# Two orders of work in a hybrid attention layer on one core: the place of one Strassen product in every pair, and the pairing of the last head's projections

## The chip, the cores and the metric

The kernel runs on one core of one Trainium2 chip. The metric is device microseconds of that core, from one launch; the median of several runs is taken. TensorE (PE in the views) does the matrix products, VectorE (DVE), ScalarE (ACT) and GpSimd (POOL) the elementwise work, SyncE (SP) issues most transfers, and POOL issues those that add to what lies in SBUF.

## The reference, cut to what matters

```python
u = rms_norm(h, norm_w)                       # 528 tokens (16 meta + 512) x 2048
proj = einsum('btd,de->bte', u, w_in)         # 2048 -> 8192 = 64 blocks of 128 columns
sb_q, sb_k, sb_v, sb_g, df_q, df_k, df_v, df_g = split(proj)   # 8 blocks (heads) each
# stick-breaking head: z = q k^T / sqrt(128); a = sigmoid(z) * running product of sigmoid(-z); o = a v
# differential head: two 64-wide softmax maps (rms norm and partial rotary on q, k), p0 - lam * p1; o = a v
mixed = concat([sb_o * silu(sb_g), subln(df_o) * silu(df_g)])
h = h + einsum('bte,ed->btd', mixed, w_out)   # 2048 -> 2048
```

Everything is float32. Queries and gates are needed for the 512 real tokens only, keys and values for all 528.

## The kernel before, in words

**Products.** A float32 product is three fp32r matmuls: each operand is split into a high part (an ACT copy, `L124`) and the rest (a DVE subtraction, `L125`), and high x high, high x low, low x high are summed in PSUM (`mm`, lines 279 to 281). Two 128-column blocks make a *pair*, and a pair is computed by a Strassen-Winograd scheme: both the weights (quadrants `a11`, `a12`, `a21`, `a22`) and the tokens (two halves) are cut in two, and seven products replace eight. The seven are called after their weights: `a11`, `a12`, `a22` as they lie, and the sums `s1` to `s4`. Each product is 8 (input side) or 7 (output side) contraction steps of 3 matmuls. `STEPS` says which PSUM bank a product goes to: `s1` to d, `a11` to a, `a12` to b, `a22` to c, `s4` to e; `s2` and then `s3` go on adding in bank a. Between `s2` and `s3` bank a has to be read: DVE adds bank d's copy to it and keeps the result as `ev_u` (line 523), and only then may PE add `s3` to the bank.

**Weights.** A pair's four quadrants come from HBM into six buffers `wr`. On the input side the sums are made by transfers that POOL issues and that add a quadrant to what lies in a buffer (`w_add`, line 174): `s1` in `a21`'s buffer right after its load, then `s2` in the same buffer once `s1` has been split, `s4` once `s2` has been split, and `s3` in `a11`'s buffer. On the output side POOL adds (line 220). A generator (`preps`, through `uses(s)`) splits each product's weights in the same order in which `proj_pair` uses the products. Each product's weights are split in two halves, and there are four buffers each for the high and low halves, so the splits run at most two products ahead of PE.

**Order.** `pairs()` lists the 32 pairs on the input side, four for each of the 8 heads (a *period*): for heads 0 to 6 differential key/value, differential query/gate, stick-breaking key/value, stick-breaking query/gate. Pairs named `..kv` are 264 columns wide per half (all 528 tokens), the others 256. Eight pairs on the output side follow: pair 32 is computed without Strassen (`direct`) while the mixed rows are read back from DRAM and split (`spread`, `combine`: tiles `uth`, `utl`, from `mr..`, `cos_t`, `sin_t`); pairs 33 to 39 are Strassen again, 7 steps deep, with a `plain` part for the last two heads, whose rows never go to DRAM.

Attention is woven into the products by `Pace`: each head is a generator that yields costs, and each step of a projection (`PACE` = 0.218 units) lets it run on. A differential head's scores `df_s` lie in two PSUM tiles in turn, so its third and later scores wait until `Exp` (line 838) has read the one before the last. In the last period (head 7) the pairs are differential key/value (28), both queries (29), stick-breaking key/value (30), both gates (31). The last differential head starts after pair 29; the stick-breaking head (`Tail`) may run only once the differential head has reached its value product (`projected`), and most of it runs inside pair 32. Pair 31's `s4` is computed at the end of its own pair; every other pair's `s4` is carried into the next pair.

A scheduler then places the instructions on each engine by its own timeline, within these dependences.

Of the kernel before, what the change touches and what calls it, by code (L numbers as in the profile page):

```python
# [2 lines left out]

# [1 line left out]

# [21 lines left out]
NH = 8  # L27
# [4 lines left out]
PACE = 0.218  # L32
# [27 lines left out]
def pairs():  # L60


    o = []
    for h in range(NH - 1):
        o += [("d_kv", h, 48 + h, 40 + h), ("d_qg", h, 56 + h, 32 + h)]
        o += [("s_kv", h, 16 + h, 8 + h), ("s_qg", h, 24 + h, h)]

    h = NH - 1
    o += [("d_kv", h, 48 + h, 40 + h), ("qq", h, h, 32 + h), ("s_kv", h, 16 + h, 8 + h), ("gg", h, 24 + h, 56 + h)]
    return o  # L70


# [10 lines left out]
def build(nc, tc, ctx, hT, win, wout, wpl, xT, prm, cst, out):  # L83
# [18 lines left out]
    def st_tile(name):  # L102
        return ww.tile([P, T], F32, tag="st", name=name, bufs=5)
# [31 lines left out]
    last_in = len(pairs()) - 1  # L135
# [90 lines left out]

    def uses(s):

        o = [(s, which) for which in ("s1", "a11", "a12", "a22", "s2", "s3")]
        if s - 1 > 1 and s - 1 not in (last_in, last_in + 1):  # L230
            o.insert(2, (s - 1, "s4"))
        if s in (last_in, len(plan) - 1):
            o.append((s, "s4"))
        return o

    def preps():
# [93 lines left out]
    for j, k in enumerate(order_h):  # L330
# [6 lines left out]
        x = ht[k]  # L337
# [348 lines left out]
        split(sk[:, 0], sk[:, 1], rk_)  # L686
        kst.append(sk)

    def sb_head(hd, kst, rv, rq_, rg):
        nm = f"sb{hd}"  # L690
        sk = kst[0]
        kh, kl = sk[:, 0], sk[:, 1]
        qh, ql = (sp.tile([P, SEQ], F32R, tag=f"dq{j}", name=f"{nm}_q{j}") for j in range(2))
        split(qh, ql, rq_[:, META:])
        yield 2
        for i in range(NB):
            n, view, spans, diag = s_views(ps_at(f"{nm}_s{i}"), i)
            qs = slice(i * P, (i + 1) * P)
            for j, (o, cs) in enumerate(spans):
                PE.matmul(o, qh[:, qs], kh[:, cs], start=True, stop=False)  # L700
                if j == len(spans) - 1:
                    PE.matmul(diag[0], msb, diag[1], start=False, stop=False)
                PE.matmul(o, qh[:, qs], kl[:, cs], start=False, stop=False)
                PE.matmul(o, ql[:, qs], kh[:, cs], start=False, stop=True)  # L704
            keep = w1_tile(f"{nm}_k{i}")[:, :n]
            beta = w3_tile(f"{nm}_b{i}")[:, :n]
            S.activation(sview(keep, i), view, AF.Sigmoid, scale=nrqs[:, i:i + 1])  # L707
            S.activation(sview(beta, i), view, AF.Sigmoid, scale=rqs[:, i:i + 1])  # L708
            run = sh_tile(f"{nm}_r{i}")[:, :n]
            V.tensor_tensor_scan(run[:, ::-1], keep[:, ::-1], ones_t.to_broadcast([P, n]), 1.0,  # L710
                                 op0=ALU.mult, op1=ALU.mult)
            V.tensor_tensor(a_t[i][:, :n - 1], beta[:, :n - 1], run[:, 1:], op=ALU.mult)  # L712
            V.memset(a_t[i][:, n - 1:n], 0.0)
            yield 1.5 if i < 3 else 2.5
        vh, vl = v_tiles(rv, nm)
        yield 1
        res = []
        last = hd == NH - 1
        yield from pv_product(vh, vl, nm, res, lambda: gate(rg[0], nm, w1_tile), hd == NH - 1, last)
        po, gs = res  # L720
        V.tensor_tensor(gs, po, gs, op=ALU.mult)
        mixed(hd, gs)
        yield 1
# [90 lines left out]
        kst.append(dk)  # L814
        yield 1

    def diff_head(hd, kst, rv, rq_, rg):
        nm = f"df{hd}"
        qst = []
        yield from diff_q(hd, rq_, qst)  # L820
# [2 lines left out]
        for i in range(NB):  # L823
            qs = slice(i * P, (i + 1) * P)
            pts = []
            sums = sp.tile([P, 2], F32, tag="sums", name=f"{nm}_sum{i}", bufs=2)
            for c in range(2):
                n, view, spans, diag = s_views(ps_at(f"{nm}_s{i}{c}"), i)
                for j, (o, cs) in enumerate(spans):
                    PE.matmul(o, qst[c][:, qs], dk[:, c, cs], start=True, stop=False)  # L830
                    if j == len(spans) - 1:
                        PE.matmul(diag[0], mdf, diag[1], start=False, stop=False)  # L832
                    PE.matmul(o, qst[c][:, qs], dk[:, 2 + c, cs], start=False, stop=True)  # L833
                mxn = sp.tile([P, 1], F32, tag="mxn", name=f"{nm}_mx{i}{c}", bufs=4)
                V.tensor_reduce(mxn, view, axis=AX.XY if i == 3 else AX.X, op=ALU.max, negate=True)  # L835
                V.tensor_tensor(mxn, mxn, rqn[:, i, c:c + 1], op=ALU.mult)  # L836
                pt = (w1_tile, w3_tile)[c](f"{nm}_p{i}{c}")[:, :n]
                S.activation(sview(pt, i), view, AF.Exp, bias=mxn, scale=rqn[:, i, c:c + 1],  # L838
                             accum_out=sums[:, c:c + 1])
                pts.append(pt)  # L840
            rec = sp.tile([P, 2], F32, tag="rec", name=f"{nm}_rec{i}", bufs=2)
            V.reciprocal(rec, sums)
            cf = sp.tile([P, 1], F32, tag="cf", name=f"{nm}_cf{i}", bufs=2)
            V.tensor_tensor(cf, rec[:, 1:2], nlam, op=ALU.mult)
            V.tensor_scalar(pts[0], pts[0], rec[:, 0:1], None, op0=ALU.mult)
            V.scalar_tensor_tensor(a_t[i][:, :n], pts[1], cf, pts[0], op0=ALU.mult, op1=ALU.add)
            yield (2.2, 3.3, 2.5, 4.5)[i]
        vh, vl = v_tiles(rv, nm)
        yield 1
        res = []  # L850
# [60 lines left out]
    def q_pair(s, *paces):  # L911
        res = [st_tile(f"o{s}{x}") for x in "ab"]
        dst = lambda e, c: place(res[e], c, True)
        for _ in second_pair(dst) if s == 1 else proj_pair(s, dst):
            step(early, *paces)
        early.drain()
        return res

    for s in range(0, last_in + 1, 4):
        hd = plan[s][1]  # L920
        kst = []
        v = kv_pair(s, kst)
        g, q = q_pair(s + 1, pace)
        if hd < NH - 1:
            pace.start(diff_head(hd, kst, v, q, [g]))
            kst = []
            v = kv_pair(s + 2, kst)
            g, q = q_pair(s + 3, pace)
            pace.start(sb_head(hd, kst, v, q, [g]))
        else:  # L930
            gates = [], []
            pace.start(diff_head(hd, kst, v, q, gates[0]))
            q, kst = g, []
            v = kv_pair(s + 2, kst)

            class Tail(Pace):
                def tick(self, n):
                    if "a" in projected:
                        Pace.tick(self, n)

            tail = Tail()
            tail.start(sb_head(hd, kst, v, q, gates[1]))
            for x, t in zip(gates[::-1], q_pair(s + 3, pace, tail)):
                x.append(t)
            projected.append("u")
            pace.drain()
            pace = tail


    def spread(k, row, x):  # L950
# [158 lines left out]
```

## Time and profile before

| | |
|---|---|
| median of 3 runs | 1060.31 us (1059.55 to 1061.11) |
| the profiled execution's own time | 1060.54 us |
| its span, first to last instruction | 1058.8 us |
| PE / DVE / ACT / POOL busy | 1017.8 / 832.1 / 631.1 / 432.2 us |
| mean granted PE clock | 0.990 |

The own time is 1.7 us above the span and 0.2 us above the median. The input side's steady part repeats every 103.1 us, one period of four pairs; the output side's Strassen pairs repeat about every 21 us. Between them lies a transition, which is looked at by itself.

### The profile page before, as it was taken

What the parts mean: (1) busy time and instruction counts of PE and PEld (TensorE: products, weight loads), DVE (VectorE), ACT (ScalarE), POOL (GpSimd) and SP (SyncE); (2) the same over time, 40 slices, a digit from 0 to 9 for tenths busy, and PEclk for the clock granted to TensorE, in tenths of its full rate; (3) what the DMA queues carried; (4) which work ended last, traced back from release to release, by engine and by line L of the source; (5) the groups of instructions that cost most, each with busy time, mean ns of one, the idle gap of its engine ahead of it and who ended that gap; (6) DMA issues with size and microseconds to landing.
All of it is one profiled execution on the core that took longest, in us unless ns stands there. A gap on an engine that the chain in (4) does not pass through costs nothing. (4 is left out here: it accounts for less than half of the span.)

```text
span 1058.8 us, 21804 instructions
## 1 busy us (share of the span) xinstructions
PE 1017.8 (96%) x8263; PEld 997.4 (94%) x8263; DVE 832.1 (79%) x1577; ACT 631.1 (60%) x1226; POOL 432.2 (41%) x374
## 2 busy tenths in 40 slices
PE   8899999999999999999999999999999987999998
PEld 7899999999999999999999999999999986899998
DVE  5978877878787878787868796878687999578766
ACT  9836665666565566566745674666566665344443
POOL 3544224323422352244224422432243265477574
PEclk9999999999999999999999999999999988999999
DMA  9346685777677767767776767676768535345431
GB/s 338 84 112 141 165 191 141 180 168 190 148 182 173 176 161 170 180 153 169 169 172 167 172 159 180 154 183 158 192 140 210 135 105 164 113 131 161 156 121 36
DMA packets 55113, 169.28 MB, mean 160 GB/s; under 512 B 6368, under 2 KB 7904, under 8 KB 55008
## 3 DMA queue, kind: packets, MB, share of 16 engines
q0 software_dynamic: 17280, 62.92, 33.9%
q1 hardware_dynamic: 37584, 104.96, 28.7%
q8 instruction: 65, 1.06, 0.4%
q14 instruction: 40, 0.33, 0.1%
q10 hardware_dynamic: 144, 0.01, 0.0%
HBM read 160.00 MB, written 7.86 MB: 159 GB/s over the span
## 5 line engine op out<-in xcount | busy, mean ns | idle before, releaser
L838 ACT ACTIVATE df_p<-df_s,df_mx,df_q_r 128x144 f32<-128x144 f32 (+3 forms) x64 | 40.2, 628 | 13.5 <-DVE df_mx L836 11.9
L749 POOL TENSOR_TENSOR df_o_r<-df_o_m,mhalf 128x8 f32<-128x8 f32 x8 | 13.7, 1714 | 57.3 <-DVE df_o_m L745 57.3
L710 DVE TENSOR_TENSOR_SCAN sb_r<-sb_k,ones 128x144 f32<-128x144 f32 (+3 forms) x32 | 29.3, 916 | 7.6 <-ACT sb_k L707 6.5
L835 DVE TENSOR_REDUCE df_mx<-df_s 128x1 f32<-128x144 f32 (+3 forms) x64 | 32.0, 500 | 3.3 <-PE df_s L833 3.3
L830 PE MATMUL df_s<-df_dk,df_qs 128*128 128x264 f32 (+3 forms) x80 | 24.4, 313 | 7.7 <-ACT df_p L838 7.7
L124 ACT ACTIVATE sb_ah<-sb_at 128x512 fp32r<-128x512 f32 (+4 forms) x40 | 18.0, 449 | 20.2 <-PE sb_at L631 18.5
L124 ACT ACTIVATE df_ah<-df_at 128x512 fp32r<-128x512 f32 (+4 forms) x40 | 17.7, 444 | 18.2 <-PE df_at L631 17.9
L707 ACT ACTIVATE sb_k<-sb_s,nrqs 128x144 f32<-128x144 f32 (+3 forms) x32 | 17.3, 541 | 17.6 <-PE sb_s L704 14.2
L830 PEld LDWEIGHTS df_s<-df_dk,df_qs 128*128 128x128 f32 x80 | 15.0, 188 | 10.4 <-ACT df_p L838 10.4
L631 PE MATMUL sb_at<-ident,a_all 128*128 128x128 f32 x112 | 20.8, 278 | 4.1 <-DVE a_all L712 4.1
L833 PE MATMUL df_s<-df_dk,df_qs 128*128 128x264 f32 (+3 forms) x80 | 23.7, 297 | 0.0
L125 DVE TENSOR_TENSOR sb_al<-sb_at,sb_ah 128x512 fp32r<-128x512 f32 (+4 forms) x40 | 20.0, 500 | 3.8 <-ACT sb_ah L124 3.4
L749 POOL TENSOR_TENSOR df_k_r<-df_k_m,mhalf 128x10 f32<-128x10 f32 x8 | 19.2, 2404 | 8.6 <-DVE df_k_m L748 8.5
L125 DVE TENSOR_TENSOR df_al<-df_at,df_ah 128x512 fp32r<-128x512 f32 (+4 forms) x40 | 19.8, 497 | 0.3
L733 POOL TENSOR_TENSOR df_q_sh<-df_q_sh,sin_t 128x512 f32<-128x512 f32 x8 | 12.4, 1552 | 18.3 <-DVE df_q_sh L732 18.3
L631 PE MATMUL df_at<-ident,a_all 128*128 128x128 f32 x112 | 19.8, 272 | 0.0
L712 DVE TENSOR_TENSOR a_all<-sb_b,sb_r 128x143 f32<-128x143 f32 (+3 forms) x32 | 18.0, 563 | 1.9
L279 PE MATMUL pj<-uth,w32a_h 128*128 128x256 f32 x56 | 16.1, 305 | 3.4 <-DVE o31b L487 3.4
L838 ACT ACT_TABLE_LOAD x7 | 9.0, 1283 | 17.5 <-DVE df_mx L836 17.5
L708 ACT ACTIVATE sb_b<-sb_s,rqs 128x144 f32<-128x144 f32 (+3 forms) x32 | 17.3, 539 | 2.8 <-DVE a_all L712 2.8
L631 PEld LDWEIGHTS sb_at<-ident,a_all 128*128 128x128 f32 x112 | 13.1, 137 | 5.8 <-DVE a_all L712 4.5
L832 PE MATMUL df_s<-zid,mdf 128*128 128x256 f32 x64 | 18.0, 281 | 0.0
(2599 smaller groups left out, 5354.3 us busy)
## 6 DMA issues: line engine op xcount, KB each, us to landing
xr<-in_xT SPq DMA_DIRECT2D x16, 256.0 KB, 3.4
out_dram<-xr SPq DMA_DIRECT2D x13, 256.0 KB, 2.0
wr0a<-in_win SPq DMA_DIRECT2D x8, 256.0 KB, 5.2
wr1a<-in_win SPq DMA_DIRECT2D x4, 512.0 KB, 7.3
wr2a<-in_win SPq DMA_DIRECT2D x4, 512.0 KB, 4.0
wr2a<-in_win POOLq DMA_DIRECT2D x4, 512.0 KB, 5.6
wr3a<-in_win SPq DMA_DIRECT2D x4, 512.0 KB, 3.5
wr3a<-in_win POOLq DMA_DIRECT2D x4, 512.0 KB, 7.1
```

Source lines behind the costliest of these rows:

```text
L124: S.activation(hi, src, AF.Copy)
L125: E.tensor_tensor(lo, src, hi.bitcast(F32), op=ALU.subtract)
L631: PE.transpose(pt[:kk, i * P:(i + 1) * P], a_t[i][:, b * P:b * P + kk], ident)
L707: S.activation(sview(keep, i), view, AF.Sigmoid, scale=nrqs[:, i:i + 1])
L710: V.tensor_tensor_scan(run[:, ::-1], keep[:, ::-1], ones_t.to_broadcast([P, n]), 1.0, op0=ALU.mult, op1=ALU.mult)
L712: V.tensor_tensor(a_t[i][:, :n - 1], beta[:, :n - 1], run[:, 1:], op=ALU.mult)
L749: G.tensor_tensor(r, m, mhalf[:, :2 * nb].rearrange("p (a c) -> p a c", c=2), op=ALU.pow)
L830: PE.matmul(o, qst[c][:, qs], dk[:, c, cs], start=True, stop=False)
L832: PE.matmul(diag[0], mdf, diag[1], start=False, stop=False)
L833: PE.matmul(o, qst[c][:, qs], dk[:, 2 + c, cs], start=False, stop=True)
L835: V.tensor_reduce(mxn, view, axis=AX.XY if i == 3 else AX.X, op=ALU.max, negate=True)
L838: S.activation(sview(pt, i), view, AF.Exp, bias=mxn, scale=rqn[:, i, c:c + 1], accum_out=sums[:, c:c + 1])
```

## The change

It does two things. In `uses(s)` the product `a22` moves behind `s2`, so that it stands between the second and the third product of bank a; in pair 31 alone `s2` also moves ahead of `a12`. And the last period's pairs become query/key of the differential head (28), differential value with stick-breaking key (29), stick-breaking value with query (30), and the gates (31). The first three of them are computed over all 528 tokens, where the queries' pair took 512 before. Their heads' generators are stepped at 1.2 times the pace, the differential head starts inside pair 29 and may wait for its value (`ready`), and the stick-breaking head starts with pair 31.

```diff
-    o += [("d_kv", h, 48 + h, 40 + h), ("qq", h, h, 32 + h), ("s_kv", h, 16 + h, 8 + h), ("gg", h, 24 + h, 56 + h)]
+    o += [("d_qkv", h, 32 + h, 40 + h), ("sd_kv", h, 48 + h, 8 + h), ("s_qkv", h, 16 + h, h), ("gg", h, 24 + h, 56 + h)]
...
-        o = [(s, which) for which in ("s1", "a11", "a12", "a22", "s2", "s3")]
+        o = [(s, which) for which in ("s1", "a11", "a12", "s2", "a22", "s3")]
...
             o.append((s, "s4"))
+        if s == last_in:
+
+            o.insert(3, o.pop(o.index((s, "s2"))))
...
-    def sb_head(hd, kst, rv, rq_, rg):
+    def sb_head(hd, kst, rv, rq_, rg, ready=lambda: True):
...
+        while not ready():
+            yield 0.3
         vh, vl = v_tiles(rv, nm)
...
+    def any_pair(s, *paces):
+
+        res = [st_tile(f"o{s}{x}") for x in "ab"]
+
+        def run():
+            for _ in proj_pair(s, lambda e, c: place(res[e], c, False), done=lambda: done.add(s)):
+                for p in paces:
+                    p.tick(1.2 * PACE)
+        return res, run
...
+            gates = [], []
+            kst, kst2 = [], []
+            qk, run = any_pair(s, pace)
+            run()
+            early.start(diff_k(hd, qk[1], kst))
+            vk, run = any_pair(s + 1, early, pace)
+            pace.gen = chain(pace.gen or (), until(lambda: kst and last_in - 3 in done, diff_head(
+                hd, kst, vk[0], qk[0], gates[0], lambda: last_in - 2 in done)))
+            run()
+            early.start(sb_keys(hd, vk[1], kst2))
+            vq, run = any_pair(s + 2, early, pace)
+            run()
+            early.drain()
...
             tail = Tail()
-            tail.start(sb_head(hd, kst, v, q, gates[1]))
+            tail.start(sb_head(hd, kst2, vq[0], vq[1], gates[1], lambda: last_in - 1 in done))
```

**Order on PE in an output pair.** The rows are PE's at the end of product `s2` (weights `w36s2`) of pair 36, first before, then after the change.

```order
L279 MATMUL pj36a_12986<-uth6_93,w36s24_h_13081 128x256
L280 MATMUL pj36a_12986<-utl6_94,w36s24_h_13081 128x256
L281 MATMUL pj36a_12986<-uth6_93,w36s24_l_13082 128x256
L279 MATMUL pj36a_12986<-uth0_81,w36s30_h_13115 128x256
L280 MATMUL pj36a_12986<-utl0_82,w36s30_h_13115 128x256
```

```order
L283 MATMUL pj36a_12990<-uth6_93,w36s24_h_13047 128x256
L284 MATMUL pj36a_12990<-utl6_94,w36s24_h_13047 128x256
L285 MATMUL pj36a_12990<-uth6_93,w36s24_l_13048 128x256
L283 MATMUL pj36c_13130<-uth0_81,w36a220_h_13081 128x256
L284 MATMUL pj36c_13130<-utl0_82,w36a220_h_13081 128x256
```

Before, `s3` follows `s2` in bank a at once; now at least 25 matmuls of bank c (`a22`) stand between them, in each of the pairs 33 to 39.

**Order on DVE beside the scores of a differential head.** The rows are DVE's around the maximum of head 6's second and third row blocks (`df6_mx11`, `df6_mx20`) in pair 26, before and after.

```order
L835 TENSOR_REDUCE df6_mx11_9726<-df6_s11_9722 128x1
L836 TENSOR_TENSOR df6_mx11_9726<-df6_mx11_9726,df6_q_r_9539 128x1
L523 TENSOR_TENSOR ev26_u_9790<-pj26a_9569,ev26_d_9567 128x264
L125 TENSOR_TENSOR w27s14_l_9563<-wr27a21_9499,w27s14_h_9562 128x512
L835 TENSOR_REDUCE df6_mx20_9806<-df6_s20_9802 128x1
```

```order
L841 TENSOR_REDUCE df6_mx11_9725<-df6_s11_9721 128x1
L842 TENSOR_TENSOR df6_mx11_9725<-df6_mx11_9725,df6_q_r_9539 128x1
L126 TENSOR_TENSOR w27s14_l_9563<-wr27a21_9499,w27s14_h_9562 128x512
L848 RECIPROCAL df6_rec1_9730<-df6_sum1_9711 128x2
L850 TENSOR_TENSOR df6_cf1_9732<-df6_rec1_9730,ones_571 128x1
L851 TENSOR_SCALAR df6_p10_9719<-df6_p10_9719,df6_rec1_9730 128x272
L852 SCALAR_TENSOR_TENSOR a_all_620<-df6_p11_9728,df6_cf1_9732,df6_p10_9719 128x272
L126 TENSOR_TENSOR w27a110_l_9595<-wr27a11_9502,w27a110_h_9594 128x512
L841 TENSOR_REDUCE df6_mx20_9806<-df6_s20_9802 128x1
```

The third block's scores come later: on PE 10 matmuls stood between scores `df6_s11` and `df6_s20` before, and 25 stand there now; the second block is finished ahead of them.

**Order on DVE in the transition.** `sb7_r` is the running product of the last stick-breaking head, `utl` the split of the mixed rows for pair 32, `w31..` are weights of pair 31. The rows show where the head's third and fourth row blocks stand, before and after.

```order
L710 SCALAR_TENSOR_TENSOR sb7_r2_11734<-sb7_k2_11730,ones_571 128x400
L125 TENSOR_TENSOR utl4_90<-sin_t_100,uth4_89 128x2x256
L712 TENSOR_TENSOR a_all_620<-sb7_b2_11731,sb7_r2_11734 128x399
L710 SCALAR_TENSOR_TENSOR sb7_r3_11774<-sb7_k3_11770,ones_571 128x528
L712 TENSOR_TENSOR a_all_620<-sb7_b3_11771,sb7_r3_11774 128x527
```

```order
L714 SCALAR_TENSOR_TENSOR sb7_r2_11529<-sb7_k2_11525,ones_571 128x400
L126 TENSOR_TENSOR w31a224_l_11304<-wr31a22_11008,w31a224_h_11303 128x512
L716 TENSOR_TENSOR a_all_620<-sb7_b2_11526,sb7_r2_11529 128x399
L126 TENSOR_TENSOR w31s30_l_11344<-wr31a11_11004,w31s30_h_11343 128x512
L714 SCALAR_TENSOR_TENSOR sb7_r3_11569<-sb7_k3_11565,ones_571 128x528
L491 TENSOR_TENSOR o31a_11365<-pj31b_11541,ev31_a_11444 128x256
L716 TENSOR_TENSOR a_all_620<-sb7_b3_11566,sb7_r3_11569 128x527
```

They stood among the last splits of pair 32's rows, at the end of that pair; now they stand among the weight splits of pair 31, a pair earlier. The head's value product (15 matmuls, five `sb7_al` splits on DVE) moves from pair 33 into pair 32.

## Rows read from the trace of the kernel before

**Rows 1.** The page: busy time by engine, and granted PE clock in 40 slices.

```profile
PE 1017.8 (96%) x8263; PEld 997.4 (94%) x8263; DVE 832.1 (79%) x1577; ACT 631.1 (60%) x1226; POOL 432.2 (41%) x374
...
PEclk9999999999999999999999999999999988999999
```

**Rows 2.** Waits of PE: what waited, for whom, us in total, times, longest.

```profile
PE df_s L830 <- ACT df_p L838: 7.7, 13, 0.9
...
PE pj31e L279 <- ACT w31s_h L124: 1.7, 1, 1.7
...
PE pj36a L279 <- DVE ev_u L523: 1.2, 1, 1.2
...
PE pj35a L279 <- DVE ev_u L523: 1.1, 1, 1.1
...
PE pj37a L279 <- DVE ev_u L523: 0.6, 1, 0.6
...
PE pj39a L279 <- ACT w39s_h L124: 0.6, 1, 0.6
```

**Rows 3.** PE in order of time, scores of head 6: start, duration, idle before.

```profile
711.86 0.39 PE L830 MATMUL df_s<-df_dk,df_qs 128*128 128x272 f32 x1 [0.32 <-ACT df_p L838]
...
715.71 0.45 PE L830 MATMUL df_s<-df_dk,df_qs 128*128 128x400 f32 x1 [0.91 <-ACT df_p L838]
```

**Rows 4.** ACT at the same place, the exponential that was waited for.

```profile
714.99 0.58 ACT L838 ACTIVATE df_p<-df_s,df_mx,df_q_r 128x272 f32<-128x272 f32 x1 [1.17 <-DVE df_mx L836]
```

**Rows 5.** Windows by stage: length, busy time (instructions) of PE, PEld, DVE, ACT, POOL; clock.

```profile
757.00:779.00 22.00, 22.00 (x183) 21.81 (x182) 18.97 (x35) 14.77 (x30) 6.95 (x7) 1.00 0.74 170
779.00:801.00 22.00, 21.87 (x191) 21.23 (x190) 15.87 (x31) 12.89 (x23) 9.39 (x8) 1.00 0.52 129
801.00:824.00 23.00, 22.53 (x185) 22.32 (x185) 18.26 (x46) 14.45 (x31) 7.29 (x6) 1.00 0.88 216
824.00:851.70 27.70, 26.04 (x216) 25.46 (x214) 26.47 (x55) 19.80 (x41) 10.25 (x11) 1.00 0.51 126
851.70:892.30 40.60, 29.92 (x217) 28.07 (x216) 38.89 (x51) 23.24 (x43) 26.32 (x22) 0.91 0.47 145
892.30:921.30 29.00, 25.88 (x168) 24.20 (x168) 18.04 (x32) 9.98 (x20) 12.06 (x11) 0.84 0.36 115
921.30:942.40 21.10, 20.49 (x172) 20.32 (x172) 16.25 (x20) 8.93 (x17) 12.97 (x11) 1.00 0.46 143
```

**Rows 6.** DVE groups of 851.7 to 892.3 us: busy, mean ns, idle before.

```profile
L125 DVE TENSOR_TENSOR utl<-mr,uth 128x512 fp32r<-128x512 f32 x7 | 7.0, 993 | 0.0
...
L710 DVE TENSOR_TENSOR_SCAN sb_r<-sb_k,ones 128x144 f32<-128x144 f32 (+3 forms) x4 | 5.4, 1345 | 0.2
L712 DVE TENSOR_TENSOR a_all<-sb_b,sb_r 128x143 f32<-128x143 f32 (+3 forms) x4 | 3.9, 980 | 0.2
...
L125 DVE TENSOR_TENSOR utl<-sin_t,uth 128x512 fp32r<-128x512 f32 x3 | 2.0, 673 | 0.0
```

**Rows 7.** The page's groups: the same two operations over all eight heads.

```profile
L710 DVE TENSOR_TENSOR_SCAN sb_r<-sb_k,ones 128x144 f32<-128x144 f32 (+3 forms) x32 | 29.3, 916 | 7.6 <-ACT sb_k L707 6.5
...
L712 DVE TENSOR_TENSOR a_all<-sb_b,sb_r 128x143 f32<-128x143 f32 (+3 forms) x32 | 18.0, 563 | 1.9
```

**Rows 8.** DVE groups of 848 to 925 us: the value product's splits.

```profile
L125 DVE TENSOR_TENSOR sb_al<-sb_at,sb_ah 128x512 fp32r<-128x512 f32 (+4 forms) x5 | 2.5, 505 | 0.8 <-ACT sb_ah L124 0.8
```

**Rows 9.** PE in order of time at the start of pair 33.

```profile
894.13 0.41 PE L279 MATMUL pj33d<-uth,w33s_h 128*128 128x256 f32 x1
894.35 0.41 PE L280 MATMUL pj33d<-utl,w33s_h 128*128 128x256 f32 x1
```

**Rows 10.** Pair 24's adding transfers: POOL's issue for s2; issue to landing of all.

```profile
641.44 1.23 POOL L174 DMA_DIRECT2D wr24a<-in_win  x1
...
DMA to landing us min/median/max: 3.4/5.6/10.5
```

**Rows 11.** ACT in order of time: first halves of pair 24's a22 and s2 split.

```profile
649.37 0.63 ACT L124 ACTIVATE w24a_h<-wr24a 128x512 fp32r<-128x512 f32 x1 [0.26 <-PE pj23e L280]
...
653.15 0.63 ACT L124 ACTIVATE w24s_h<-wr24a 128x512 fp32r<-128x512 f32 x1 [1.72 <-PE pj24b L280]
```

More of the change, by code (lines that the diff above doesn't have):

```diff
@@ L2 @@
 from contextlib import ExitStack
+from itertools import chain
 import numpy as np
@@ L815, in diff_k, with diff_head @@
         yield 1
-    def diff_head(hd, kst, rv, rq_, rg):
+    def diff_head(hd, kst, rv, rq_, rg, ready=lambda: True):
         nm = f"df{hd}"
@@ L847, in diff_head @@
             yield (2.2, 3.3, 2.5, 4.5)[i]
+        while not ready():
+            yield 0.3
         vh, vl = v_tiles(rv, nm)
@@ L917, in q_pair, with until @@
         return res
+    def any_pair(s, *paces):
[5 more added lines that the diff above has]
+        return res, run
+    done = set()
+    def until(test, gen):
+        while not test():
+            yield 0.3
+        yield from gen
     for s in range(0, last_in + 1, 4):
         hd = plan[s][1]
[L921 to L930, printed above, removed]
-            gates = [], []
-            pace.start(diff_head(hd, kst, v, q, gates[0]))
-            q, kst = g, []
-            v = kv_pair(s + 2, kst)
+        if hd == NH - 1:
+            gates = [], []
+            kst, kst2 = [], []
[10 more added lines that the diff above has]
+            early.drain()
             class Tail(Pace):
@@ L947, in build @@
             pace = tail
+            break
+        kst = []
+        v = kv_pair(s, kst)
+        g, q = q_pair(s + 1, pace)
+        pace.start(diff_head(hd, kst, v, q, [g]))
+        kst = []
+        v = kv_pair(s + 2, kst)
+        g, q = q_pair(s + 3, pace)
+        pace.start(sb_head(hd, kst, v, q, [g]))
     def spread(k, row, x):
```

## The prediction, made before the changed kernel was run

> **What bounds the kernel now.** I read the page first. PE is busy for 1017.8 of 1058.8 us, and the granted clock falls below nine tenths in two slices only, the 33rd and 34th of 40 [rows 1]. So the kernel is bound by PE, and a change that adds or removes next to no matmuls can gain only what PE loses in waits, or in time at the lower clock. The list of PE's waits is short [rows 2], and three places matter.
>
> First, the scores of the differential heads: 7.7 us in 13 waits. PE in order of time shows a pair of them in a period, 0.32 us before the second row block's first score and 0.91 us before the third's [rows 3]. The same two come back every 103.1 us in six periods (6 x 1.2 = 7.4, and a single one of about 0.4 in the last period). The third block needs the PSUM tile that the exponential at 714.99 reads, and PE stands ready before that has ended at 715.57 [rows 4].
>
> Second, the output pairs: PE waits for `ev_u` between the second and the third product of bank a, 1.2 us in pair 36, 1.1 in 35, 0.6 in each of 34, 37 and 38. Pairs 33 and 39 show 0.6 us at the same place under the name of a weight split [rows 2].
>
> Third, the transition between input and output side. The windows say what bounds it [rows 5]: in an undisturbed output pair 172 matmuls take 20.49 us, 0.119 us each. From 851.7 to 892.3 us PE has 217 matmuls, 25.8 us at that rate, in 40.6 us, and DVE is busy for 38.89 of these: this stage is DVE's. From 892.3 to 921.3 PE has 168 matmuls, 20.0 us of work, in 29.0; the value product of the last stick-breaking head stands in between, and the clock is 0.84.
>
> **The change part by part.** *Scores.* Between the second block's last scores and the third's there are 25 matmuls where there were 10. 15 x 0.119 = 1.8 us, which is more than the 0.91 that PE waited [rows 3]. The way from the first block to the second is 31 matmuls long before and after, so the 0.3 us there stays. Gain: 6 x 0.9 = 5.5 us. Bounds: nothing, if another wait takes its place, and 7.4 if both go. DVE gets the second block's finishing operations ahead of the third's maximum; they are short and are done within the 1.8 us.
>
> *Output pairs.* `ev_u` is now made while PE works on bank c, 25 x 0.119 = 3.0 us, and the longest wait was 1.2 [rows 2]. Sum: 0.6 + 1.1 + 1.2 + 0.6 + 0.6 = 4.1, and 0.6 each for pairs 33 and 39, if these were `ev_u` too, as their place says: 5.3 us. Bounds 4.1 and 5.3. On the input side nothing of this was waited for: there the scheduler already put other matmuls between the two products.
>
> *Transition, up to the end of pair 32.* The running products and their multiplications leave it: 5.4 + 3.9 = 9.3 us of DVE [rows 6]. In come the value product's five splits, 2.5 us [rows 8], and the multiplication and the split of the head's own result and a small split of v, some 1.6 us by the splits of that size at 0.67 us [rows 6]. Three pairs of 528 tokens add five small DVE instructions, 0.6 us by an estimate of 0.12 each. The moved work must find room earlier. The stretch from 824 to 851.7 has none, 26.47 of 27.70 [rows 5]; but the differential head's own work moves up by most of a pair, and the three stretches ahead of it have 3.0 + 6.1 + 4.7 = 13.9 us idle. I therefore count DVE's work over the whole way. From 757 to 892.3 it is busy for 18.97 + 15.87 + 18.26 + 26.47 + 38.89 = 118.5 us and idle for 16.8. Afterwards it has 118.5 + 2.5 + 1.6 + 0.6 = 123.2. If a third of the idle time gets filled, 11 to 12 us stay, and pair 32 ends at 757 + 123.2 + 11.5 = 892: **where it ended before**. The bounds are no filling at all (897, a loss of 5) and all but 5 us filled (885, a gain of 7). I take the middle, since the work moves exactly into stretches with room, but in an order that ties it to PE. What PE gains and loses before that point is hidden behind DVE: pair 31's 1.7 us for `s4` [rows 2], whose adding transfer now has three products to land in; about 0.6 us for 8 more columns in 168 matmuls (8/256 of 20 us); some 5 us of the head's scores.
>
> *Transition, pair 33.* The 168 matmuls lose the 27 of the value product: 141 remain, 16.8 us at 0.119. In the run before, PE started this pair at half clock, 0.22 us from matmul to matmul [rows 9]; that should happen again, since PE still waits for DVE ahead of it: some 20 matmuls at 0.1 us more, 2 us. With 0.7 us for first waits the stretch takes 19.5 us instead of 29.0: **a gain of 9.5 us**. PE's wait for the head's end, here 27 matmuls strung on ACT and DVE, is what goes. Bounds: 6 (weight splits late) and 12 (full clock, no wait).
>
> *Port.* In the transition the same 128x512 split takes 0.67 us for one tile and 0.99 on the mean for another, and the scans 1.345 us on the mean against 0.916 over all heads [rows 6, 7], while POOL is busy for 26.32 of 40.60 us there and 7.29 of 23.00 in the stretch from 801 [rows 5]. If the moved work takes the mean of all heads, it shrinks by 4 x (0.43 + 0.42) = 3.4 us, which the sum leaves out. The Trainium skill (Advanced Engine Details and Errata, VectorE Performance Modes) says that GpSimd shares VectorE's second SBUF port and that the two block each other; by it the moved work would shrink in the same way, and the time would be some 3 us lower than my sum. The trace agrees in kind; the moved work does, however, also meet rope's POOL operations in its new place.
>
> *Sum.* 1060.5 (the profiled execution's own) - 5.5 - 5.3 - 0 - 9.5 = 1040.2. The median is 0.2 us lower, so **1040 us**.
>
> **The rivals.** *The transition gives nothing.* The tighter steps put scores, transposes and value products of head 7 next to each other, with few matmuls between a tile's making and its use, so PE waits in pairs 29 to 31; and DVE fills no idle time, so that pair 32 ends 5 us later, and pair 33 wins only 6. For it: DVE at 26.47 of 27.70 in pair 31 [rows 5]. Against: the room ahead of it. 1060.5 - 10.8 - 1 = 1049.
>
> *The scores wait elsewhere.* The third block's two scores are now 9 matmuls apart where they were 23, so the second of them may wait for its own exponential, one ACT instruction of 0.58 us behind the first's [rows 4]. 1.1 us lie between, so I think it is just covered. 1046.
>
> *The transition gives more.* DVE fills all but 5 us, or its work shrinks as under *Port*: 1034 to 1037.
>
> *Slower: the sum of s2 lands too late.* `s2`'s weights are now split one product earlier, in all 27 pairs from 4 to 30, and the transfer that makes them can't start earlier. In pair 24 it is issued at 641.44 and its like take 5.6 us on the median and 10.5 at most [rows 10]: 647.0 or 651.9. `a22`'s split, whose place it takes, is at 649.37; the old place is 653.15 [rows 11]. So the median lands with 2.3 us to spare and the worst is 2.6 us late. The splits run up to two products ahead of PE, 2 x 24 x 0.119 = 5.7 us, so this should not reach PE. It decides if PE loses 20.3 / 27 = 0.75 us per pair, that is, if landings were some 4 us later than the worst of these. Then 1060 and above; at 2 us per pair 1094.
>
> *No effect.* All three kinds of wait come back next to where they were: 1060.
>
> **How the numbers follow.** The forecast (1035 to 1046 by its own bounds) 0.50; transition gives nothing 0.17; scores wait elsewhere 0.12, at the edge of that; transition gives more 0.11; slower 0.06; no effect 0.04. The range from 1033 to 1051 leaves out the last two and the tails of the others. About 0.2% is what a measurement of this kernel can tell from no change: faster 0.90, same 0.04, slower 0.06.
>
> **What the changed profile would show.** Right: no wait for `ev_u` in the output pairs, which come every 20.4 us instead of 21.1; one wait of some 0.3 us per period at the scores, and periods of 102.2 us; pair 33's first matmul near 892 less what the periods gained, its third product of bank a some 19 to 20 us later, and no value product in it. Wrong: waits of PE for `df_al`, `sb_al`, `df_p` or weight splits in pairs 29 to 31; periods of 103 us; waits for `w..s` splits in every pair, with ACT standing before them until an adding transfer lands.

## The result, and the profile after

The changed kernel takes 1048.34 us on the median of 4 runs (1046.98 to 1051.62), the kernel before 1060.64: a ratio of 0.9887, interval [0.9874, 0.99]. That is 12.3 us less; 20 were forecast. Its profiled execution is its shortest run: 1046.98 us, span 1045.2, so between the two profiled executions the difference is 13.6 us.

The page after: busy time by engine, and the granted clock of PE in 40 slices [rows 1].

```profile
PE 1013.2 (97%) x8263; PEld 994.8 (95%) x8263; DVE 827.0 (79%) x1581; ACT 628.7 (60%) x1226; POOL 442.1 (42%) x374
...
PEclk9999999999999999999999999999999998999999
```

PE was idle for 41.0 us of its span and is idle for 32.0 now. Its waits, whole span: what waited, for whom, us in total, times, longest [rows 2].

```profile
PE pj L284 <- DVE utl L126: 3.6, 3, 2.6
PE df_s L836 <- ACT df_p L844: 3.0, 6, 0.5
...
PE sb_at L635 <- DVE vl L126: 2.3, 1, 2.3
PE sb_at L658 <- DVE sb_al L126: 2.1, 1, 2.1
PE df_bo L768 <- POOL df_o_r L755: 2.1, 1, 2.1
...
PE pj7a L285 <- DVE w7s_l L126: 0.7, 1, 0.7
...
PE pj19a L285 <- DVE w19s_l L126: 0.6, 1, 0.6
```

No wait for `ev_u` is left. The scores' 13 waits (7.7 us) became 6 (3.0). New are one wait each around the value products of the last two stick-breaking heads (`sb_at`, in pairs 28 and 31), one for POOL's result `df_o_r`, and small ones for the low half of `s2`'s weights in bank a.

PE in order of time at head 6's scores [rows 3]: start, duration, idle before. The second block still waits, 0.49 us instead of 0.32; the third no longer does.

```profile
709.39 0.39 PE L836 MATMUL df_s<-df_dk,df_qs 128*128 128x272 f32 x1 [0.49 <-ACT df_p L844]
...
714.01 0.34 PE L836 MATMUL df_s<-df_dk,df_qs 128*128 128x400 f32 x1
```

Now the windows by stage [rows 5]: from head 6's wait to pair 33's first matmul; pairs 28 to 31; pair 32; pair 33; output pair 35. Columns are length, then busy time (instructions) of PE, PEld, DVE, ACT, POOL, then the granted clock, the DMA engines' busy share and GB/s.

```profile
709.39:896.26 186.87, 173.35 (x1368) 168.73 (x1369) 155.54 (x308) 115.05 (x230) 76.30 (x63) 0.97 0.61 156
...
741.55:857.14 115.59, 110.55 (x912) 108.69 (x909) 93.48 (x196) 74.43 (x149) 39.06 (x32) 1.00 0.67 160
857.14:896.26 39.12, 30.83 (x206) 28.84 (x205) 34.04 (x47) 19.22 (x37) 28.97 (x24) 0.87 0.40 130
896.26:916.48 20.22, 19.66 (x165) 19.25 (x163) 15.99 (x25) 8.13 (x15) 14.22 (x11) 1.00 0.53 168
...
936.68:956.86 20.18, 20.18 (x174) 20.18 (x172) 15.53 (x22) 9.63 (x19) 15.75 (x13) 1.00 0.48 156
```

The same stretches of the kernel before: from head 6's wait to pair 33, pair 33, and pair 32.

```profile
711.86:892.30 180.44, 166.58 (x1342) 162.62 (x1343) 153.93 (x295) 113.72 (x225) 72.40 (x63) 0.98 0.64 160
892.30:923.86 31.56, 28.43 (x189) 26.76 (x189) 19.61 (x34) 10.50 (x21) 12.72 (x11) 0.85 0.38 121
...
855.36:892.31 36.95, 29.66 (x214) 28.02 (x215) 35.24 (x44) 21.36 (x40) 25.23 (x20) 0.92 0.44 137
```

So the stretch ahead of pair 33 is 6.4 us longer and pair 33 is 11.3 us shorter. PE's idle time ahead of pair 33 stayed (13.9 us before, 13.5 after) while its busy time grew by 6.8. There are 26 more matmuls in it, as 24 have left pair 33 with the value product; at 0.119 us each they are 3.1 us, and the rest is longer busy time of the others, some of it at the lower clock (0.97 against 0.98). The account of the two profiled executions:

| Term | Predicted | Measured |
|---|---|---|
| start of the span to head 6's score wait | -4.6 (five of six periods and the start) | -2.5 |
| from there to pair 33 | -0.9 (sixth period), transition 0 | +6.4 |
| pair 33, its 0.6 for `ev_u` included | -10.1 | -11.3 |
| pair 34 to the end | -4.7 | -6.2 |
| sum | -20.3 | -13.6 |

The last row but one is 134.9 us before and 128.7 after. Of the new part of the change, 4.9 us are left (6.4 - 11.3). Whether even these belong to the new part, two traces cannot say; the experiments can.

Pair 32 is 2.2 us longer than before, but no longer DVE's: DVE works 34.04 of 39.12 us, where it worked 35.24 of 36.95. POOL in order of time there: start, duration, idle before.

```profile
857.46 2.88 POOL L601 TENSOR_TENSOR o31b<-o31b,rstd 128x512 f32<-128x512 f32 x1 [3.52 <-DVE o31b L491]
...
865.15 1.74 POOL L604 TENSOR_TENSOR o31b<-o31b,df_sg 128x512 f32<-128x512 f32 x1
...
879.61 0.94 POOL L274 TENSOR_TENSOR mr6a<-mr6a,mr6b 128x256 f32<-128x256 f32 x1 [3.42 <-DMA mr6b<-mixd]
...
889.77 1.67 POOL L755 TENSOR_TENSOR df_o_r<-df_o_m,mhalf 128x8 f32<-128x8 f32 x1
891.42 0.71 POOL L277 TENSOR_TENSOR sin_t<-sin_t 128x256 f32<-128x256 f32 x1
```

And the end of DVE's work there, which waits for an ACT copy that waits for POOL's last sum.

```profile
892.84 1.09 DVE L126 TENSOR_TENSOR utl<-sin_t,uth 128x512 fp32r<-128x512 f32 x1 [4.31 <-ACT uth L125]
```

POOL has the four gate multiplications (8.1 us together, two of them shown) ahead of the sums that make the operands, and PE's last wait in the pair is for `df_o_r` (2.1 us). That gave the first theory: *POOL's queue took DVE's place in pair 32.* Its rivals: *DVE's total work sets the end*, as predicted, and *the tighter steps cost in pairs 28 to 31 what pair 33 gains*.

### The profile page after: what moved, and what is told of

It reads as the page before. It is cut to its first block, busy times and chain, and to the rows that moved or that the text cites. A ratio compares the mean times of both kernels' runs of the same rounds, so it can differ in the third digit from the quotient of the medians.

```text
span 1045.2 us, 21825 instructions
## 1 busy us (share of the span) xinstructions
PE 1013.2 (97%) x8263; PEld 994.8 (95%) x8263; DVE 827.0 (79%) x1581; ACT 628.7 (60%) x1226; POOL 442.1 (42%) x374
## 5 line engine op out<-in xcount | busy, mean ns | idle before, releaser
L755 POOL TENSOR_TENSOR df_k_r<-df_k_m,mhalf 128x10 f32<-128x10 f32 x8 | 16.4, 2047 | 16.4 <-DVE df_k_m L754 16.3
L635 PE MATMUL sb_at<-ident,a_all 128*128 128x128 f32 x112 | 20.3, 277 | 2.3 <-DVE vl L126 2.3
L284 PE MATMUL pj<-utl,w32a_h 128*128 128x256 f32 x56 | 17.4, 322 | 3.6 <-DVE utl L126 3.6
L852 DVE SCALAR_TENSOR_TENSOR a_all<-df_p,df_cf,df_p 128x144 f32<-128x144 f32 (+3 forms) x32 | 19.4, 607 | 0.2
L285 PE MATMUL pj<-uth,w32a_l 128*128 128x256 f32 x56 | 16.9, 316 | 1.3 <-DVE w32a_l L126 1.3
```

Source lines behind the costliest of these rows:

```text
L284: PE.matmul(o, w[0], u[1], start=False, stop=False, skip_group_check=more)
L635: PE.transpose(pt[:kk, i * P:(i + 1) * P], a_t[i][:, b * P:b * P + kk], ident)
L755: G.tensor_tensor(r, m, mhalf[:, :2 * nb].rearrange("p (a c) -> p a c", c=2), op=ALU.pow)
```

## The experiments

**The parts by themselves.** Four kernels, each with one part or with one cost moved. First, the order of products on one side, in the kernel before.

```diff
-        o = [(s, which) for which in ("s1", "a11", "a12", "a22", "s2", "s3")]
+        o = [(s, which) for which in ("s1", "a11", "a12", *(("s2", "a22") if s <= last_in else ("a22", "s2")), "s3")]
...
+        if s == last_in:
+            o.insert(3, o.pop(o.index((s, "s2"))))
```

> The kernel before, with a22 behind s2 on the input side alone (and s2 ahead of a12 in pair 31, as in the change). By the prediction's term for the scores: six periods of 0.9 us less, so 1055.1 against 1060.6. By the trace of the changed kernel, whose periods came every 102.35 to 102.9 us instead of 103.08 (0.5 on the mean): about 3 us less, 1057.5, with the 0.9 us wait before the third block's scores gone and new waits of up to 0.65 us for the low half of s3's weights in some pairs. By a rival, in which the periods' gain comes from the changed last period alone: no change, 1060.6.

Measured: 1055.66 us against 1060.73, ratio 0.9955 [0.9943, 0.9967]: 5.1 less. The waits of PE:

```profile
PE df_s L833 <- ACT df_p L841: 3.0, 6, 0.5
...
PE pj7a L284 <- DVE w7s_l L125: 0.2, 1, 0.2
```

From the first head's score wait to the seventh's, PE in order of time:

```profile
195.71 0.39 PE L833 MATMUL df_s<-df_dk,df_qs 128*128 128x272 f32 x1 [0.49 <-ACT df_p L841]
...
707.63 0.39 PE L833 MATMUL df_s<-df_dk,df_qs 128*128 128x272 f32 x1 [0.50 <-ACT df_p L841]
```

Five periods in 511.92 us are 102.38 each, 0.7 less than the 103.1 of before; six of them 4.2 us. PE's busy time in a period is 101.70 us in both kernels, and its idle time falls from 1.38 to 0.70: the 0.9 us wait goes, the first wait is 0.2 longer, and 0.2 for split weights are new, the same in pairs 7, 11, 15, 19, 23 and 27; the rest lies in gaps that the list of waits does not show. These weights are `s2`'s, not `s3`'s as the expectation has it: the wait stands at the second product of bank a. In the changed kernel's profiled execution two of these waits were 0.6 and 0.7, which is part of why it showed less. Its pair 7, PE, ACT and DVE in order of time; ACT comes to the high half without idle time before it, DVE waits for ACT's half, then takes 3.18 us for two splits, beside two POOL instructions:

```profile
217.72 0.39 PE L285 MATMUL pj7a<-uth,w7s_l 128*128 128x256 f32 x1 [0.65 <-DVE w7s_l L126]
```

```profile
215.56 1.14 ACT L125 ACTIVATE w7s_h<-wr7a 128x512 fp32r<-128x512 f32 x2
```

```profile
216.21 3.18 DVE L126 TENSOR_TENSOR w7s_l<-wr7a,w7s_h 128x512 fp32r<-128x512 f32 x2 [0.62 <-ACT w7s_h L125]
```

The rival (no gain in the steady periods) is out.

Second, the same edit with `s > last_in` and without the second hunk.

> The kernel before, with a22 behind s2 on the output side alone. By the prediction: no wait for ev_u in pairs 33 to 39, 4.1 to 5.3 us less, so 1055.3 to 1056.5. By the changed kernel's trace (20.2 us per output pair instead of 21.1 to 21.7, pair 39 shorter by 0.8): 6 to 7 us less, 1054. If pair 33's wait of 0.6 us has another cause than ev_u, its 0.6 us stay.

Measured: 1054.36, ratio 0.9941 [0.9929, 0.9953]: 6.4 less. Its profile has no wait for `ev_u`, pairs 34 to 37 come every 20.2 us, and the 0.6 us in pairs 33 and 39 are gone too, so these were `ev_u`'s, as the prediction took them to be. The waits summed to 5.3 us; 6.4 were gained, since a wait in these pairs costs more than its idle time. The output side's last row of before has 20.49 us of PE busy in 21.10 [rows 5]; in the changed kernel pair 35 has 20.18 in 20.18. A wait of 0.6 us cost 0.9.

Third, the changed kernel with the old order of products, so the new pairs and their steps alone.

```diff
-        o = [(s, which) for which in ("s1", "a11", "a12", "s2", "a22", "s3")]
+        o = [(s, which) for which in ("s1", "a11", "a12", "a22", "s2", "s3")]
...
-        if s == last_in:
-            o.insert(3, o.pop(o.index((s, "s2"))))
```

> The changed kernel with the products in their old order on both sides: of the change, the new pairs of the last period and their tighter steps alone. By the prediction's terms (transition 0, pair 33 9.5 us less): 1051. By what the changed kernel's trace leaves for it (transition 6.4 us longer, pair 33 shorter by 11.3 less 0.6 for ev_u): some 4 to 5 us less, 1056. If the two parts help each other, more than 1058, so that the three parts alone do not add up to the 12.3 us of the whole.

Measured: 1063.36, ratio 1.0032 [1.002, 1.0043]: 2.6 **more** than before. Neither number expected, and the third sentence holds: the parts alone sum to -5.1 - 6.4 + 2.6 = -8.9, the whole gives -12.3. Its waits of PE, among others:

```profile
PE sb_at L658 <- ACT sb_ah L125: 2.5, 1, 2.5
PE pj31e L283 <- ACT w31s_h L125: 1.9, 1, 1.9
...
PE pj30a L283 <- DVE ev_u L527: 1.6, 1, 1.6
```

Fourth, the first theory's test: the last head's gates on DVE, in the changed kernel.

```diff
     def gate(g, nm, w_tile):
-        gf = g[:, META:]
-        G.tensor_tensor(gf, gf, rstd[:, META:], op=ALU.mult)
+        gf, E = g[:, META:], V if nm in (f'sb{NH - 1}', f'df{NH - 1}') else G
+        E.tensor_tensor(gf, gf, rstd[:, META:], op=ALU.mult)
...
-        G.tensor_tensor(gf, gf, sg, op=ALU.mult)
+        E.tensor_tensor(gf, gf, sg, op=ALU.mult)
```

> The changed kernel with the four multiplications of the last head's two gates on DVE instead of POOL: 8.1 us of POOL work in pair 32 become some 2.9 us of DVE work. Theory 1, that pair 32 is now set by POOL's queue (these four stand ahead of the combining sums, and DVE's splits took up to 2.35 us for two instead of 0.67 each while they ran): pair 32 gets 3 to 5 us shorter, 1044 to 1045. Rival, the prediction's own view that DVE's total sets the end of pair 32: 2.9 us longer, 1051.

Measured: 1048.36, ratio 0.9885 [0.9872, 0.9898]: no change against the changed kernel. Windows of pairs 28 to 31, pair 32, pair 33:

```profile
740.97:858.06 117.09, 112.08 (x911) 110.19 (x909) 94.74 (x196) 74.66 (x149) 38.40 (x32) 0.99 0.65 158
858.06:893.06 35.00, 28.75 (x206) 26.92 (x205) 32.78 (x48) 18.05 (x35) 20.99 (x19) 0.90 0.41 131
893.06:916.13 23.07, 20.36 (x162) 19.54 (x163) 19.59 (x27) 8.72 (x18) 14.71 (x13) 1.00 0.53 166
```

Pair 32 is 4.1 us shorter, as theory 1 said, and pair 33 is 2.9 longer; PE waits there for weights split on DVE:

```profile
PE pj33a L285 <- DVE w33a_l L126: 1.3, 1, 1.3
PE pj33d L285 <- DVE w33s_l L126: 0.9, 2, 0.8
```

Pairs 28 to 31 were 1.5 us longer in this execution, at a clock of 0.99 and without a new wait. So POOL's queue did lengthen pair 32 in the changed kernel, but with the gates alone moved the time came back one pair later. The theory does not say where the 8 us went.

**What the new pairs are worth, and the steps.** First, the new order on both sides, `s2` ahead in pair 31, the last period as before.

> The kernel before with the whole of the new order of products (input side, output side, s2 ahead in pair 31) and the last period as it was. If the two orders add up (5.1 and 6.4 us less, measured alone): 1049.2, and then the new pairs of the last period give only about 1 us of the change's 12.3 instead of the prediction's 9.5. If the new pairs are worth what the two traces show between the last steady period and pair 34 (6.4 us longer, 11.3 less 0.6 shorter): 4.3, so 1052.6. If the parts simply add, with the new pairs' 2.6 us of loss measured alone: 1045.7.

Measured: 1048.22 against 1061.05, ratio 0.9877 [0.9863, 0.9891]: 12.8 less, as much as the whole change. **The new pairs with their tighter steps brought nothing.** Windows of pairs 28 to 31, 32 and 33:

```profile
741.33:845.13 103.80, 103.80 (x871) 103.09 (x869) 85.26 (x178) 68.08 (x137) 37.43 (x32) 1.00 0.70 173
845.13:885.30 40.17, 28.67 (x220) 26.27 (x218) 39.75 (x51) 22.98 (x44) 29.19 (x24) 0.95 0.45 142
885.30:917.03 31.73, 27.81 (x188) 26.30 (x189) 21.60 (x35) 10.52 (x22) 13.18 (x11) 0.85 0.36 113
```

Here PE is busy for all 103.80 us of pairs 28 to 31. Against it the changed kernel has 11.8 us more there (6.75 of busy time, 5.0 of waits), 1.1 less in pair 32 and 11.5 less in pair 33. What pair 33 won was paid nearly in full, and 5.0 of the price are waits.

Second, the new order on the input side without `s2` ahead of `a12` in pair 31 (the first experiment without its second hunk).

> The kernel before with a22 behind s2 on the input side, but without s2 ahead of a12 in pair 31. If the first run's 5.1 us came from the scores alone (prediction: 5.5): 1055.6, as there. If the periods gave 6 x 0.68 = 4.1 us, as that run's trace reads, and the rest came from pair 31, where PE no longer waited 1.7 us for s2's weights: 1056.6 to 1057.5.

Measured: 1056.03, ratio 0.9947 [0.9935, 0.996], not to be told from the first experiment's 0.9955 [0.9943, 0.9967]. PE does not wait for `w31s` in this run either. So the one edit of pair 31 has no effect that this measurement shows.

Third and fourth, the steps at the ordinary pace, in pair 28 alone and in all three pairs.

```diff
-                    p.tick(1.2 * PACE)
+                    p.tick((1.0 if s == last_in - 3 else 1.2) * PACE)
```

> The changed kernel with pair 28 stepped at the ordinary pace (1.0 instead of 1.2). Theory, that the tighter steps there put two groups of transposes and a value product of the last steady head next to each other, so that PE waits 2.27 us for the split of v between them: that wait goes, 1046. Rival, that the work put off comes back as a wait in pairs 29 to 32: 1048 or more.

Measured: 1044.18, ratio 0.9839 [0.9825, 0.9852], 4.2 us less than the changed kernel, more than the 2.27 expected, and the rival is out. Windows as above:

```profile
740.56:851.58 111.02, 108.89 (x905) 107.74 (x902) 92.05 (x194) 74.85 (x150) 37.03 (x32) 1.00 0.67 163
851.58:890.69 39.11, 31.62 (x211) 29.15 (x211) 29.55 (x46) 17.53 (x35) 32.33 (x24) 0.83 0.40 130
890.69:911.47 20.78, 19.91 (x164) 19.42 (x163) 16.64 (x27) 8.48 (x17) 13.97 (x11) 1.00 0.56 175
```

Pairs 28 to 31 are 4.6 us shorter, pair 32 is the same, pair 33 0.6 longer. The waits of 2.27 us in pair 28 and of some 0.7 in pair 30 are gone; where pair 31 had 2.09 for `sb_al`, it has 0.9 for a weight split.

```diff
-                    p.tick(1.2 * PACE)
+                    p.tick(1.0 * PACE)
```

> The changed kernel with pairs 28, 29 and 30 all stepped at the ordinary pace. If the tighter steps cost more than they bring in all three pairs (waits of 2.27, 0.47 and 0.22 us): 1045.5. If they are what brings the last head's work ahead of pair 32: the stick-breaking head ends later, PE's waits in pairs 32 and 33 grow by some 3 us, 1050.

Measured: 1043.45, ratio 0.983 [0.9816, 0.9843], 4.9 us less than the changed kernel. Windows:

```profile
740.24:847.08 106.84, 106.76 (x889) 105.82 (x886) 90.62 (x189) 71.32 (x142) 35.64 (x32) 1.00 0.67 169
847.08:890.72 43.64, 32.30 (x216) 30.86 (x216) 37.92 (x51) 21.65 (x42) 30.13 (x24) 0.84 0.44 137
890.72:912.69 21.97, 20.77 (x177) 20.54 (x175) 16.68 (x28) 9.11 (x18) 13.94 (x11) 1.00 0.41 127
```

Both sentences come true, with the first larger: against the changed kernel, pairs 28 to 31 get 8.8 us shorter (3.8 of busy time, 5.0 of waits), of which pair 32 takes back 4.5 and pair 33 1.8. So behind the new order the new pairs are worth 4.8 us, and the tighter steps take all of it away; those of pair 28 alone take 4.2.

**Gates on DVE, with the ordinary pace.** The edit of the fourth experiment on top of the two last ones.

> The changed kernel with pair 28 at the ordinary pace and the last head's four gate multiplications on DVE. In the run with the pace alone, DVE was busy for only 28.4 of 38 us in pair 32 and POOL for 27.4, with one POOL sum stretched to 6.45 us and PE's waits 8.7 us. If POOL's queue sets pair 32 there: 3 us less than with the pace alone, 1041. If the time is given back in pair 33, as when the gates moved in the changed kernel (4.1 us gained, 2.9 and more lost behind): 1044.

Measured: 1042.64, ratio 0.9823 [0.981, 0.9837]: 1.5 us less than without the gates' move, with intervals that overlap. Its pair 32 is 37.41 us instead of 39.11 and pair 33 unchanged at 20.8.

> The changed kernel with pairs 28 to 30 at the ordinary pace and the last head's four gate multiplications on DVE. DVE was busy for 32.3 of 38 us there, and PE's longest wait (5.1 us) was for a split at the end of DVE's queue. If DVE sets the end of pair 32 here: 2 us longer than with the pace alone, 1045.5. If POOL does: 1041.

Measured: 1040.09, ratio 0.9807 [0.9793, 0.982]: the fastest kernel of this study, 8.2 us ahead of the changed one and 3.4 of the one with the pace alone (2.4 by the two ratios, whose intervals touch; each of its runs is faster than each of that kernel's). Windows:

```profile
741.16:848.24 107.08, 106.76 (x889) 105.83 (x886) 90.48 (x189) 71.18 (x142) 35.64 (x32) 1.00 0.69 169
848.24:888.90 40.66, 32.44 (x223) 30.62 (x224) 35.57 (x57) 21.87 (x43) 21.61 (x20) 0.83 0.46 139
888.90:909.13 20.23, 19.71 (x167) 19.50 (x166) 16.64 (x26) 8.61 (x16) 14.87 (x11) 1.00 0.51 163
```

DVE has six more instructions in pair 32, four of them the gates', and 2.4 us less busy time than without the move (35.57 against 37.92; over all three stages 142.7 against 145.2): with 8.5 us of POOL gone, its own instructions got shorter. Here the gates on POOL, and what they do to DVE, are a cost, and nothing is given back. In pair 32 PE is still idle for 8.2 us, 5.8 of them at once, for one ACT copy:

```profile
PE pj L283 <- ACT uth L125: 5.8, 1, 5.8
```

What stands behind that copy was not looked into by an experiment.

**Why the new pairs alone lost.** The new pairs at the ordinary pace, with the old order of products everywhere (the third experiment with the last edit of the pace).

> The new pairs of the last period at the ordinary pace, with the old order of products. If the new pairs by themselves bring 4.8 us (1048.2 for the new order alone less 1043.45 with them at this pace) and add to the order: 1056. If they need the new order, without which a sum of a weight split comes too late in these pairs (1.6 us for ev_u in pair 30, 1.9 us for s2's weights in pair 31 in the earlier run): 1058.5 to 1060.

Measured: 1059.97, ratio 0.9992 [0.9983, 1.0001]. The tighter steps' cost shows here too (1063.36 with them), but without the new order the new pairs bring about 0.7 us (by the interval, from 1.8 less to 0.1 more). So they need it. Where, the last run asked, with `s2` ahead in pair 31 as in the change:

```diff
+        o = [(s, which) for which in ("s1", "a11", "a12", *(("s2", "a22") if last_in - 3 <= s <= last_in else ("a22", "s2")), "s3")]
```

> The new pairs of the last period at the ordinary pace, and the new order of products in these four pairs alone; the other input pairs and the output pairs keep the old order. With the old order everywhere the new pairs brought 0.7 us. If they need the new order inside the last period itself: 4 to 5 us less than before, 1056. If their gain of 4.8 us behind the new order everywhere came from the output pairs' order or from the steady pairs': 1059 to 1060, as with the old order.

Measured: 1057.38, ratio 0.9969 [0.9957, 0.998]: 3.9 less than before, between the two expectations and nearer the first. The order's own gain in these four pairs is about 0.9 of it (5.1 of the first experiment less six periods of 0.7), so the new pairs bring some 3 of the 4.8 us with the new order in the last period alone, where they bring 0.7 without it. What the rest depends on stays open, and the interval is 1.2 us to either side.

## Why the prediction was right in kind and 8 us too low

The forecast of 20.3 us less was 10.8 for the order of products and 9.5 for the last period's new pairs. The order alone gave 12.8, and the new pairs as the change steps them gave nothing. So the direction was right because of the order, and the 8 us that are missing lie in the last period.

Seven kernels with the new order of products on both sides, us by stage in one profiled execution each; the last column is the median of the runs, from which these executions stand off by 0.1 to 1.4 us:

| Kernel | pairs 28 to 31 | pair 32 | pair 33 | sum | median |
|---|---|---|---|---|---|
| new order alone | 103.80 | 40.17 | 31.73 | 175.70 | 1048.2 |
| the change | 115.59 | 39.12 | 20.22 | 174.93 | 1048.3 |
| gates on DVE | 117.09 | 35.00 | 23.07 | 175.16 | 1048.4 |
| pair 28 at ordinary pace | 111.02 | 39.11 | 20.78 | 170.91 | 1044.2 |
| the same, gates on DVE | 111.00 | 37.41 | 20.79 | 169.20 | 1042.6 |
| all at ordinary pace | 106.84 | 43.64 | 21.97 | 172.45 | 1043.5 |
| the same, gates on DVE | 107.08 | 40.66 | 20.23 | 167.97 | 1040.1 |

- **The order of products: right.** 5.5 + 5.3 = 10.8 us were forecast, 12.8 came by the runs with both. The scores gave 4.2 where the term says 5.5: the third block's wait went, the second block's grew by 0.2, and `s2`'s weights came late by 0.2 in each period. The sentence that the second block's wait of 0.3 us "stays" was wrong by that. The other 0.9 of the input side's 5.1 lies behind the sixth period and was not taken apart. The output side gave 6.4 where the term says 5.3, because the term took the idle time alone.
- **The slower rival, `s2` too late: it is there, and small.** One pair in four waits for `s2`'s low half, 0.2 us in the first experiment and up to 0.7 in the changed kernel. That is some 0.05 to 0.1 us per pair where 0.75 would have decided, and the link that is late in the rows above is DVE's split, with ACT's ahead of it: ACT did not wait for the sum's landing.
- **Pair 33: right, mis-sized.** 9.5 forecast, 11.3 less 0.6 measured. Its half-clock start did not come; the pair's clock is 1.00 in the window above. The lower clock did not go altogether: pair 32's is 0.87 where the order alone has 0.95, so part of what pair 33 won there was paid a pair earlier.
- **The transition up to the end of pair 32: the step that failed.** The term was 0 with bounds of 5 and -7, and it measured +6.4; against the run with the order alone it is +10.7. The count of DVE's work was not the fault: DVE's busy time from head 6's wait to pair 33 rose by 1.6 us, against 4.7 counted. *Port* named 3.4 us less; the running products and their multiplications took 6.9 us where they had taken 9.3. The fault is the sentence "What PE gains and loses before that point is hidden behind DVE." It holds only for pair 32 of the kernel before. In the first three stretches of pairs 28 to 31 PE was busy for 22.00 of 22.00, 21.87 of 22.00 and 22.53 of 23.00 us [rows 5], and in the run with the order alone for all of 103.80. Matmuls that are moved there add their length, whatever room DVE has. At the ordinary pace 18 more matmuls stand in pairs 28 to 31 than with the order alone, and they get 3.0 us longer; pair 32 gets 3.5 us longer, so against the order alone the term would have been +6.5 even so. The tighter steps make it 41 more matmuls and 6.75 us of busy time (4.9 at 0.119 each; the rest was not taken apart), and 5.0 us of waits that the ordinary pace does not have. DVE's idle time, of which a third was to be filled, grew from 26.5 to 31.3.
- **What then held pair 32 at 39 us** was not DVE's total: with the gates off POOL and on DVE, pair 32 falls by 4.1, 1.7 and 3.0 us at the three paces, one execution each. So POOL's queue and what it does to DVE, the thing that the sum had set aside, is part of it; the rest is open. At the changed kernel's own pace the gain came back in pair 33, at the other two it did not; why not, the runs do not separate.
- **The rivals.** "The transition gives nothing", at 1049, comes nearest: it named waits in pairs 29 to 31 between tile and use, which are there (0.47 and 0.22 us in pair 30, 2.09 in pair 31, and 2.27 already in pair 28). The one for `sb_al` in pair 31 is also what the prediction had named as a sign that it was wrong. But the rival charged the waits against a pair 33 that wins only 6; in truth pair 33 became as short as the pairs behind it, and PE's moved work, which no rival names, was the rest of the price. So its 1049 is near in part by luck. That the fastest kernel, with the ordinary pace and the gates on DVE, takes the 1040 us of the forecast is luck too: the order gave 2 us more than its term, and the transition was not 0.

## What to carry to other kernels

Before work is moved from a stage where the busiest engine waits, read that same engine's share in the stage that takes it in: where PE is 99% busy, moved matmuls cost their full length, and only the waits and the time at the lower clock that vanish are a gain. Weaving a serial chain in more tightly than its slowest link allows puts its latencies on PE one by one; here the ordinary pace gained 3 to 5 us over 1.2 times it. And test the parts alone and together: here one part gave all of the change's gain, the other needed the first to be worth anything, and its own tuning number had cancelled it.

## What the runs showed of the hardware that was not expected

A wait of PE can cost more than its idle time. Output pairs with one wait of 0.61 us took 21.08 to 21.10 us, without it 20.2: 0.9.

```profile
942.38 0.36 PE L279 MATMUL pj34a<-uth,w34s_h 128*128 128x256 f32 x1 [0.61 <-DVE ev_u L523]
```

PE's busy time also falls, from 20.49 to 20.18 with as many matmuls. In the rows, a matmul lasts 0.28 us and the next starts 0.12 after it; the one behind a gap lasts 0.36, and the one ahead of it has nothing to share the engine with. On the input side, where a wait went and another came, PE's busy time stayed at 101.70 us a period.

DVE and POOL hold each other up, and either can be the one that is slowed. In the changed kernel with pair 28 at the ordinary pace, one POOL sum of 128x256, whose like on that line take 0.73 to 1.18 us in this pair, shows 6.45, from 854.15 to 860.60:

```profile
854.15 6.45 POOL L276 TENSOR_TENSOR mr<-mr 128x256 f32<-128x256 f32 x1
```

In just that time DVE runs twelve instructions without a gap, each split at its shortest, the last one ending at 860.49:

```profile
854.11 0.67 DVE L126 TENSOR_TENSOR w32a_l<-wr32a,w32a_h 128x512 fp32r<-128x512 f32 x1
...
859.93 0.56 DVE L126 TENSOR_TENSOR sb_al<-sb_at,sb_ah 128x400 fp32r<-128x400 f32 x1
```

In the changed kernel it goes the other way: two splits take 2.35 us while POOL works without a break, and the same split 0.68 at 877.47, where POOL waits for a load.

```profile
868.79 2.35 DVE L126 TENSOR_TENSOR utl<-mr,uth 128x512 fp32r<-128x512 f32 x2
...
877.47 0.68 DVE L126 TENSOR_TENSOR utl<-mr,uth 128x512 fp32r<-128x512 f32 x1
```

The Trainium skill (Advanced Engine Details and Errata, GPSIMD Details) says that the Pool engine shares a read and a write interface with DVE and conflicts with DVE instructions that read two inputs from SBUF; the splits and the sums of the mixed rows here are such, and the trace agrees. (The section that the prediction names, VectorE Performance Modes, says it of VectorE's two-port instructions.) Which of the two loses, these sections leave open, and these runs show both.
